# A key's low part copied or subtracted twice, and the values' weights split on VectorE instead of GpSimd

## The chip, the cores and the metric

The kernel runs on one core of a Trainium2 chip. Its metric is the device time of one execution in microseconds (us), given as the median of several runs. Besides the runs there is one profiled execution, whose trace has every instruction of every engine: TensorE (PE in the profile, with its weight loads as PEld), VectorE (DVE), ScalarE (ACT), GpSimd (POOL) and the queue that issues the transfers (SP).

## The reference

Two layers work on 512 latent tokens with a prefix of 256 context tokens, all 1024 wide. Layer 0 mixes tokens with attention, layer 1 with a state space scan in two directions, and each is followed by a gated feed-forward part with a short convolution. The change lies in the attention of layer 0:

```python
q_l, k_l, v_l = jnp.split(h_lat @ w_qkv, [Q_DIM, Q_DIM + KV_DIM], axis=-1)
q_l = rms_norm(q_l.reshape(bsz, seq, N_HEADS, HEAD_DIM), q_norm)
k_l = rms_norm(k_l.reshape(bsz, seq, N_KV_HEADS, HEAD_DIM), k_norm)
q_l = apply_rope(q_l, cos, sin)
k_l = apply_rope(k_l, cos, sin)
...
k_all = jnp.concatenate([k_l, k_c], axis=1)
v_all = jnp.concatenate([v_l, v_c], axis=1)
# per block of queries: softmax(q k^T / 8) v, with 16 query heads on 4 key heads of 64
```

Latent queries see all 768 keys, context queries the 256 of the context. Everything is float32.

## The kernel before

**Numbers in two parts.** TensorE works on a rounded type (fp32r). To keep float32 accuracy each operand is split into a high part, which is a rounded copy of it made on ScalarE (a cast), and a low part, which is the operand minus the high part. `split` (lines 81 to 87) does both: the cast on ScalarE is L85, the subtraction is L87, on VectorE or, with `lo_engine="pool"`, on GpSimd. `mm3` (L105, L106, L108) then adds three matmuls: high by high, high by low, low by high. `load_w` transfers one tile of weights of 128 by 1024 from HBM (L95, issued by SP) and splits it; the tile and its two parts (`wst`, `wh`, `wl`) come out of one pool of ten buffers that is also used by the modulation's weights (`wada`) and the queries' weights (`wq`).

**Who sets the order.** A first section of `attention` is ordered by hand (`manual_schedule`, for PE, ACT and DVE). In it the modulation of the latent and context tokens (L312 on VectorE, L321 on ScalarE, L322 on VectorE, for each of eight rows of 128 channels) runs one row ahead of the projections of the keys and the first queries (`k_step`, six accumulators `ps_l`). All other instructions are put in order by a planner, engine by engine, by when it expects their inputs to be there and by their place in the program; each engine and each DMA queue then works strictly in that order. `pin=True` in `load_w` adds `keep_in_program_order` to the cast and the subtraction: each then has to follow the instruction that was traced before it on its engine.

**After the hand-ordered section.** A loop over six tiles (`for n, j in enumerate(...)`, L744 on) projects the context tokens into one PSUM bank each (`ps_c`, matmuls as `k_step`) and copies the bank out on ScalarE (L748). A pool of four banks serves `ps_c`, the sums of squares of the norms (`ssq`, L567) and later the values (`ps_v`). Into this loop the program puts other work: the two tiles of the values' weights (`wv`), and from n = 1 and n = 2 on the first keys and the first queries (`early`), one step of each per turn.

`keys` and `queries` share `normed`: squares on ScalarE (L558), the gain (L559), a swap of halves by four transfers (L562, `qsw`), sums on TensorE (L567), the rotary product on VectorE (L569, L570, L571), the inverse root in three steps on ScalarE (L576, L577, L578), its correction on VectorE (L580) and the products L581 and L582. `queries` ends with a `split` of 768 columns. `keys` ends with the part that the change touches: a key head lies in one half of the partitions (`s`), and the scores need it in both halves. For each of the two heads of a tile, ScalarE writes the high part to its own half and to the other one (L593, L594), VectorE subtracts the low part in its own half (L595), and ScalarE copies that to the other half (L596). `keys` runs twice: for tile 0 in the loop above, and for tile 1 in the middle of attention (`chain["k"]`).

Behind the loop come the values (`values`, L547: 24 matmuls for each of six tiles of tokens, copied out by L549), between which the row maxima of the first pair of heads are put (`maxima`, L651 on TensorE, L653 on VectorE); the maxima read the queries' and the keys' high parts. Then attention proper follows, eight pairs of heads in seven steps each, with the later queries, the modulation of the later parts and the output projection woven in by costs.

Of the kernel before, what the change touches and what calls it, by code (L numbers as in the profile page):

```python
# [11 lines left out]
ALU = mybir.AluOpType  # L12
# [55 lines left out]
def t3(g, name, dt=F32, n=T):  # L68
    return g.t3p.tile([P, n], dt, tag="t3", bufs=g.n3, name=name)


def t4(g, name, dt=F32):
    return g.p.tile([P, 1024], dt, tag="t4", bufs=10, name=name)


def _r(ap):

    return ap.bitcast(F32)


def split(g, src, hi, lo, lo_engine="dve", pin=False):

    nc = g.nc
    keep = g.tc.keep_in_program_order if pin else lambda i: i
    keep(nc.scalar.copy(hi, src))  # L85
    eng = nc.vector if lo_engine == "dve" else nc.gpsimd
    keep(eng.tensor_tensor(lo, src, _r(hi), ALU.subtract))  # L87


def load_w(g, dram, lo_engine="dve", pin=False):  # L90

    st = t4(g, "wst")
    wh = t4(g, "wh", F32R)
    wl = t4(g, "wl", F32R)
    g.nc.sync.dma_start(st, dram)  # L95
    split(g, st, wh, wl, lo_engine=lo_engine, pin=pin)
    return wh, wl
# [312 lines left out]
def attention(g, adas, project, X):  # L410


    nc, I = g.nc, g.I
# [77 lines left out]
    def k_step(m, j, out, h):  # L491
        ks = slice(j * P, (j + 1) * P)
        mm3(g, tuple(w[:, ks] for w in slabs[m]), [(out, h[m])], m == 0, m == KT - 1)
# [42 lines left out]
    wv = []  # L536
# [18 lines left out]
    def normed(qs, gain):  # L555

        sq = t3(g, "qsq")
        nc.scalar.activation(sq, qs, AF.Square)  # L558
        nc.scalar.activation(qs, qs, AF.Identity, scale=gain)  # L559
        sw = t2("qsw")  # L560
        for b in range(4):
            nc.sync.dma_start(sw[32 * (b ^ 1) : 32 * (b ^ 1) + 32], qs[32 * b : 32 * b + 32, :L])  # L562
        ss = []
        for c0, c1 in ((0, L), (L, T)):
            ps = Bk("ssq")
            for s in S64:
                nc.tensor.matmul(ps[s, : c1 - c0], g.ones[s, :HD], sq[s, c0:c1], start=True, stop=True)  # L567
            ss.append((ps[:, : c1 - c0], slice(c0, c1)))
        nc.vector.tensor_tensor(qs[:, :L], qs[:, :L], g.cos, ALU.mult)  # L569
        nc.vector.tensor_tensor(sw, sw, g.sin, ALU.mult)  # L570
        nc.vector.tensor_tensor(qs[:, :L], qs[:, :L], sw, ALU.add)  # L571
        yield

        y, u = t3(g, "qy"), sq
        for ps, c in ss:
            nc.scalar.activation(y[:, c], ps, AF.Ln, scale=1.0 / HD, bias=eps64)  # L576
        nc.scalar.activation(y, y, AF.Exp, scale=-0.5)  # L577
        nc.scalar.activation(u, y, AF.Square)  # L578
        for ps, c in ss:
            nc.vector.scalar_tensor_tensor(u[:, c], ps, HD * EPS, u[:, c], ALU.add, ALU.mult)  # L580
        nc.vector.tensor_tensor(qs, qs, y, ALU.mult)  # L581
        nc.vector.scalar_tensor_tensor(qs, u, -3.0 * HD, qs, ALU.add, ALU.mult)  # L582
        yield
# [3 lines left out]
    def keys(j, qs):  # L587
        yield from normed(qs, kn)
        for e in range(2):

            h, l = t3(g, f"kh{j}{e}", F32R), t3(g, f"kl{j}{e}", F32R)
            s, o = S64[e], S64[1 - e]
            nc.scalar.copy(h[s], qs[s])  # L593
            nc.scalar.copy(h[o], qs[s])  # L594
            nc.vector.tensor_tensor(l[s], qs[s], _r(h)[s], ALU.subtract)  # L595
            nc.scalar.copy(l[o], _r(l)[s])  # L596
            k2[2 * j + e] = (h, l)

    qprep = {}
# [1 line left out]
    def queries(p, qs):  # L601
        yield from normed(qs(), g.qn8)
        qprep[p] = t3(g, "qh", F32R), t3(g, "ql", F32R)
        split(g, qs(), *qprep[p])
# [139 lines left out]
    for n, j in enumerate((0, 1, 2, 4, 5, 3)):  # L744
        ps = Bk("ps_c")
        for k in range(KT):
            k_step(k, j, ps[:, :C], hc)
        nc.scalar.copy(raw[j][:, L:], ps[:, :C])  # L748
        if n in (1, 3):
            wv.append(load_w(g, I["wv"][len(wv)], lo_engine="pool", pin=True))  # L750
        if n in (1, 2):
            early.append(keys(0, raw[0]) if n == 1 else queries(0, lambda: raw[1]))
        for gen in early:
            next(gen, None)
# [5 lines left out]
    for p, j in ((1, 2), (2, 4), (3, 5)):  # L760
        qraw[p] = raw[j]
    chain = {p: queries(p, lambda p=p: qraw[p]) for p in range(1, 8)}
    chain["k"] = keys(1, raw[3])

    g.oT = {}
# [603 lines left out]
def body(nc, tc, I, out, dbg=None):  # L1369
# [36 lines left out]
    def project(fs, wo):  # L1406

        for i in range(2):
            for m in range(KT):
                down(g, [wo[f] for f in fs], [g.oT[f] for f in fs], g.mod[0][2], streams, x, [[(i, 0, streams[i][0])]], ms=[m])  # L1410
                yield len(fs) * (0.69 if i == 0 else 0.36)

    attention(g, adas, project, X)
    g.tables = True
    nrm = Norm(g, 0, 4, 3, streams, "f0")
# [135 lines left out]
```

## Time and profile before

| | |
|---|---|
| median of 3 runs | 1911.2 us (1906.7 to 1911.81) |
| profiled execution, its own time | 1909.82 us |
| its span, first to last instruction | 1908.0 us |
| granted clock of TensorE over the span | 0.995 |
| busy: PE, DVE, ACT, POOL | 1864.2, 1321.9, 844.5, 263.8 us |
| HBM traffic | 198.79 MB read, 6.82 MB written, 108 GB/s |

How to read the rows: a row of the order of work gives the start in us from the span's beginning, the duration, the engine, the line of the kernel, the operation, and its output and input tiles by name. What stands in square brackets is how long the engine was idle before it, and what ended that. "x2" are two instructions of a kind in a row, with one common duration. A row of a stretch gives its bounds and length, then the busy time (and count) of PE, PEld, DVE, ACT and POOL, the granted clock as a share of full speed, the busy share of the DMA engines, and GB/s. Matmuls overlap, so that the single ones look longer than the distance from one to the next.

### The profile page before, as it was taken

The page shows a single profiled execution, that of the slowest core. Times are in us where ns is not written, and L with a number is a line of the kernel's source. Part 1 is how long each engine was busy: PE and PEld are TensorE (multiplying, and loading weights), DVE is VectorE, ACT ScalarE, POOL GpSimd, SP SyncE. Part 2 cuts the span into 40 slices and gives each one's busy share as a digit, 9 for nine tenths or more (in the row PEclk, how much of TensorE's full clock was granted, in tenths as well). Part 3 has the DMA queues.
Part 4 walks back from the last instruction along what each step waited for, and adds up shares of the span by engine and source line. Part 5 has one row for each costly group of instructions (what it writes and reads, how often), then busy time and mean ns, then how long its engine had stood idle before and what let it go on. Part 6 is the DMA issues. An engine that isn't in the chain of part 4 may idle for free.

```text
span 1908.0 us, 27239 instructions
## 1 busy us (share of the span) xinstructions
PE 1864.2 (98%) x10696; PEld 1527.1 (80%) x10696; DVE 1321.9 (69%) x1953; ACT 844.5 (44%) x1446; POOL 263.8 (14%) x246
## 2 busy tenths in 40 slices
PE   8899999989999999999989999999999999999999
PEld 6674546588888888888888888888888878888887
DVE  5578989678777777544488867777788466565555
ACT  3645644354122222222266677776666352323331
POOL 2200000031000000000040344344334210000000
PEclk8999999999999999999999999999999999999999
DMA  9123341014433555222223434434443223323232
GB/s 338 56 71 106 111 150 55 7 56 167 136 124 121 174 187 175 67 67 67 66 79 103 116 108 122 122 111 133 122 143 111 89 78 90 99 88 111 88 100 89
DMA packets 73424, 210.00 MB, mean 110 GB/s; under 512 B 8912, under 2 KB 14416, under 8 KB 73168
## 3 DMA queue, kind: packets, MB, share of 16 engines
q1 hardware_dynamic: 73296, 208.26, 35.0%
q8 instruction: 84, 1.38, 0.3%
q14 instruction: 44, 0.36, 0.1%
HBM read 198.79 MB, written 6.82 MB: 108 GB/s over the span
## 4 chain that ended last, share of the span: by engine, by line
PE 79%; DVE 9%; issue 4%; ACT 2%; POOL 1%; DMA 1%; SPq 0%; DVEq 0%; POOLq 0%; ACTq 0%
PE ps_up L106 10%; PE ps_up L108 10%; PE ps_up L105 10%; PE ps_d L105 6%; PE ps_d L108 6%; PE ps_d L106 6%; PE ps_in L108 4%; PE ps_in L106 4%; PE ps_in L105 4%; PE ps_o L687 2%; PE ps_s L723 2%; PE ps_st L1147 2%; DVE ht L312 1%; PE ps_wo L108 1%; PE ps_wo L105 1%
## 5 line engine op out<-in xcount | busy, mean ns | idle before, releaser
L87 DVE TENSOR_TENSOR wl<-wst,wh 128x1024 fp32r<-128x1024 f32 x209 | 260.4, 1246 | 243.3 <-PE ps_up L106 137.5
L85 ACT CAST wh<-wst 128x1024 fp32r<-128x1024 f32 x211 | 221.2, 1049 | 426.5 <-DMA wst<-in_wup 336.9
L106 PE MATMUL ps_up<-hlf,wh 128*128 128x512 f32 x1008 | 357.0, 354 | 0.0
L105 PE MATMUL ps_up<-hhf,wh 128*128 128x512 f32 x1008 | 356.9, 354 | 0.0
L108 PE MATMUL ps_up<-hhf,wl 128*128 128x512 f32 x1008 | 356.8, 354 | 0.0
L105 PEld LDWEIGHTS ps_up<-hhf,wh 128*128 128x128 f32 x1008 | 190.6, 189 | 26.5
L108 PEld LDWEIGHTS ps_up<-hhf,wl 128*128 128x128 f32 x1008 | 190.5, 189 | 26.4
L106 PEld LDWEIGHTS ps_up<-hlf,wh 128*128 128x128 f32 x1008 | 190.6, 189 | 26.2
L105 PE MATMUL ps_in<-hhs,wh 128*128 128x512 f32 (+1 forms) x560 | 204.4, 365 | 0.0
L106 PE MATMUL ps_in<-hls,wh 128*128 128x512 f32 (+1 forms) x560 | 199.4, 356 | 0.0
L108 PE MATMUL ps_in<-hhs,wl 128*128 128x512 f32 (+1 forms) x560 | 198.7, 355 | 0.0
L105 PE MATMUL ps_d<-hdh,wh 128*128 128x512 f32 (+1 forms) x568 | 193.6, 342 | 1.4 <-DVE X L897 1.2
L108 PE MATMUL ps_d<-hdh,wl 128*128 128x512 f32 (+1 forms) x568 | 193.5, 341 | 0.0
L106 PE MATMUL ps_d<-hdl,wh 128*128 128x512 f32 (+1 forms) x568 | 193.0, 340 | 0.3 <-DVE hdl L87 0.3
L897 DVE SCALAR_TENSOR_TENSOR X<-ps_d,mod,X 128x512 f32<-128x512 f32 (+1 forms) x224 | 124.9, 583 | 34.1 <-PE ps_d L108 33.6
L106 PEld LDWEIGHTS ps_d<-hdl,wh 128*128 128x128 f32 x568 | 106.6, 188 | 14.9 <-DVE hdl L87 0.7
L105 PEld LDWEIGHTS ps_d<-hdh,wh 128*128 128x128 f32 x568 | 106.3, 188 | 14.8 <-DVE X L897 1.4
L105 PEld LDWEIGHTS ps_in<-hhs,wh 128*128 128x128 f32 x560 | 105.9, 189 | 15.1 <-issue 1.0
L108 PEld LDWEIGHTS ps_in<-hhs,wl 128*128 128x128 f32 x560 | 105.8, 189 | 14.8
L108 PEld LDWEIGHTS ps_d<-hdh,wl 128*128 128x128 f32 x568 | 106.7, 188 | 13.1
L106 PEld LDWEIGHTS ps_in<-hls,wh 128*128 128x128 f32 x560 | 106.0, 189 | 13.2
L726 ACT ACTIVATE pr<-ps_s 128x1024 f32<-128x1024 f32 x56 | 57.1, 1020 | 97.5 <-PE ps_s L725 95.6
(341 smaller groups left out, 3493.7 us busy)
## 6 DMA issues: line engine op xcount, KB each, us to landing
wst<-in_wup SPq DMA_DIRECT2D x88, 512.0 KB, 3.6
wada<-in_adaT SPq DMA_DIRECT2D x56, 512.0 KB, 4.0
wst<-in_win SPq DMA_DIRECT2D x48, 512.0 KB, 3.7
wst<-in_wdown SPq DMA_DIRECT2D x44, 512.0 KB, 4.1
E<-ad SPq DMA_DIRECT2D x64, 256.0 KB, 6.8
wada<-in_adaB SPq DMA_DIRECT2D x24, 512.0 KB, 4.9
ec<-ead SPq DMA_DIRECT2D x64, 128.0 KB, 5.4
wst<-in_wout SPq DMA_DIRECT2D x16, 512.0 KB, 3.6
```

What stands on the lines that cost most here:

```text
L85: keep(nc.scalar.copy(hi, src))
L87: keep(eng.tensor_tensor(lo, src, _r(hi), ALU.subtract))
L105: mm(out, wh, ah, start=first, stop=False)
L106: mm(out, wh, al, start=False, stop=False)
L108: mm(out, wl, ah, start=False, stop=last)
L312: nc.vector.scalar_tensor_tensor(t[:, c0:c1], ap, g.moda[layer][ca][:, m, v : v + 1], rs[:, c0:c1], ALU.mult, ALU.mult)
L687: nc.tensor.matmul(po[S64[e], :n], v, pr[:, 512 * e + off : 512 * e + off + n], start=first, stop=last)
L723: nc.tensor.matmul(outs[e], a[S64[e], k], b[S64[e], q], start=i == 0, stop=False)
L726: nc.scalar.activation(pr, ps, AF.Exp)
L897: nc.vector.scalar_tensor_tensor(ap, o[:, c0:c1], gate[:, m, v : v + 1], ap, ALU.mult, ALU.add)
L1147: nc.tensor.matmul(ps[:, d * 256 : (d + 1) * 256], Bt[:, t * P : (t + 1) * P], xw[d][t], start=t == ts[0], stop=t == ts[-1])
```

## The change

For the half of the partitions that a key does not lie in, the low part is subtracted on VectorE a second time, from the same inputs, instead of being copied there by ScalarE. In the loop over the context tiles, the two loads of the values' weights stand at n = 3 and n = 5 instead of 1 and 3, their subtraction is on VectorE instead of GpSimd, and neither cast nor subtraction is pinned.

```diff
@@ -592,8 +592,8 @@
             s, o = S64[e], S64[1 - e]
             nc.scalar.copy(h[s], qs[s])
             nc.scalar.copy(h[o], qs[s])
-            nc.vector.tensor_tensor(l[s], qs[s], _r(h)[s], ALU.subtract)
-            nc.scalar.copy(l[o], _r(l)[s])
+            for to in (s, o):
+                nc.vector.tensor_tensor(l[to], qs[s], _r(h)[s], ALU.subtract)
             k2[2 * j + e] = (h, l)
 
@@ -746,8 +746,8 @@
         for k in range(KT):
             k_step(k, j, ps[:, :C], hc)
         nc.scalar.copy(raw[j][:, L:], ps[:, :C])
-        if n in (1, 3):
-            wv.append(load_w(g, I["wv"][len(wv)], lo_engine="pool", pin=True))
+        if n in (3, 5):
+            wv.append(load_w(g, I["wv"][len(wv)]))
         if n in (1, 2):
             early.append(keys(0, raw[0]) if n == 1 else queries(0, lambda: raw[1]))
         for gen in early:
```

## The prediction

> **What bounds the kernel.** I read the busy times first, then the busy times of short stretches around the changed lines, then the order of work on each engine there.
>
> ```profile
> PE 1864.2 (98%) x10696; PEld 1527.1 (80%) x10696; DVE 1321.9 (69%) x1953; ACT 844.5 (44%) x1446; POOL 263.8 (14%) x246
> ```
>
> TensorE is busy for 98% of the span. A change on VectorE, ScalarE or GpSimd is therefore worth only the time that TensorE waits for those engines. The stretches show one such wait beside the change (PE, PEld, DVE, ACT and POOL busy, then the granted clock):
>
> ```profile
> 88.25:93.91 5.66, 0.00 (x0) 0.00 (x0) 1.84 (x4) 5.52 (x9) 0.00 (x0) 0.97 0.00 1
> 93.91:98.31 4.40, 4.40 (x24) 4.27 (x24) 4.25 (x6) 2.73 (x4) 0.00 (x0) 0.65 0.00 0
> 98.31:118.66 20.35, 19.80 (x149) 16.72 (x149) 15.95 (x23) 8.70 (x14) 0.00 (x0) 1.00 0.25 75
> ```
>
> TensorE does nothing for 5.66 us, while ScalarE works through nearly all of it. Then 24 matmuls of the values run at a clock of 0.65. From 98.31 on TensorE is nearly full again. The first matmul after the gap says what it waited for:
>
> ```profile
> 93.91 0.58 PE L547 MATMUL ps_v<-wh,hha 128*128 128x256 f32 x1 [5.66 <-ACT raw L748]
> ```
>
> It needs a PSUM bank that holds a finished context projection, and ScalarE's copy (L748) frees it. The copy is late because of what stands ahead of it on ScalarE:
>
> ```profile
> 82.62 0.83 ACT L593 CAST kh<-raw 64x768 fp32r<-64x768 f32 x1 [3.66 <-DVE raw L582]
> 83.36 0.36 ACT L748 COPY raw<-ps_c 128x256 f32<-128x256 f32 x1
> 83.62 1.05 ACT L85 CAST wh<-wst 128x1024 fp32r<-128x1024 f32 x1
> 84.70 0.83 ACT L594 CAST kh<-raw 64x768 fp32r<-64x768 f32 x1
> 88.29 0.83 ACT L596 CAST kl<-kl 64x768 fp32r<-64x768 f32 x1 [2.76 <-DVE kl L595]
> 89.13 0.83 ACT L593 CAST kh<-raw 64x768 fp32r<-64x768 f32 x1
> 89.99 0.83 ACT L594 CAST kh<-raw 64x768 fp32r<-64x768 f32 x1
> 90.83 1.05 ACT L576 ACTIVATE qy<-ssq,eps 128x512 f32<-128x512 f32 x2
> 91.90 0.83 ACT L596 CAST kl<-kl 64x768 fp32r<-64x768 f32 x1
> 92.76 0.84 ACT L577 ACTIVATE qy<-qy 128x768 f32<-128x768 f32 x1
> 93.51 0.35 ACT L748 COPY raw<-ps_c 128x256 f32<-128x256 f32 x1
> ```
>
> The first copy of a low part (L596) waits 2.76 us for VectorE's subtraction L595. Everything behind it on ScalarE waits too, the copy at 93.51 among it. VectorE and GpSimd at that time:
>
> ```profile
> 83.89 0.69 DVE L569 TENSOR_TENSOR raw<-raw,cs 128x512 f32<-128x512 f32 x1 [1.36 <-DMA qsw<-raw]
> 84.50 0.68 DVE L570 TENSOR_TENSOR qsw<-qsw,cs 128x512 f32<-128x512 f32 x1
> 85.11 3.15 DVE L595 TENSOR_TENSOR kl<-raw,kh 64x768 fp32r<-64x768 f32 x1
> 88.19 0.67 DVE L571 TENSOR_TENSOR raw<-raw,qsw 128x512 f32<-128x512 f32 x1
> 90.00 0.96 DVE L595 TENSOR_TENSOR kl<-raw,kh 64x768 fp32r<-64x768 f32 x1 [1.14 <-ACT kh L593]
> 93.63 0.96 DVE L581 TENSOR_TENSOR raw<-raw,qy 128x768 f32<-128x768 f32 x1 [2.68 <-ACT qy L577]
> 94.70 1.02 DVE L580 SCALAR_TENSOR_TENSOR qsq<-ssq,qsq 128x512 f32<-128x512 f32 x2
> 95.76 0.96 DVE L582 SCALAR_TENSOR_TENSOR raw<-qsq,raw 128x768 f32<-128x768 f32 x1
> ```
>
> ```profile
> 84.81 2.64 POOL L87 TENSOR_TENSOR wl<-wst,wh 128x1024 fp32r<-128x1024 f32 x1 [7.58 <-ACT wh L85]
> ```
>
> The same subtraction takes 3.15 us beside GpSimd's L87 and 0.96 us alone, and it ends when that L87 has ended (85.11 + 3.15 = 88.26; 84.81 + 2.64 = 87.45). So all three parts of the edit stand in this wait: ScalarE's L596, GpSimd's L87, and ScalarE's L85 at 83.62.
>
> **The change, part by part.** I follow two chains to 98.31, where the maxima of the first pair start on TensorE: the PSUM bank for the first values, and the first query's high part, which the maxima read.
>
> ScalarE, up to the bank. Gone are L85 at 83.62 (84.70 - 83.62 = 1.08), the wait and the first L596 (89.13 - 85.53 = 3.60, where L594 ends at 84.70 + 0.83), and the second L596 (92.76 - 91.90 = 0.86): 5.54 us. The copy then ends at 93.86 - 5.54 = 88.32 where it ended at 93.86. TensorE has finished its own work at 88.25, so 0.1 us of the 5.66 is left.
>
> The clock. With no gap, the 24 matmuls need 4.40 x 0.65 = 2.86 us, and end at 88.35 + 2.86 = 91.2.
>
> VectorE, up to the query. It now has four L595 (3.84 us at 0.96) where two were. Its work from the first high part (82.62 + 0.83 = 83.45) on is these, the three rotary steps L569 to L571 (0.69 + 0.68 + 0.67 = 2.04), L581 (0.96), L580 (1.02) and L582 (0.96): 8.82 us, to 92.3. L577 on ScalarE, which L581 needs, ends by 92.76 + 0.84 - 5.54 = 88.1, and L581's turn comes at 83.45 + 3.84 + 2.04 = 89.3, so ScalarE is no longer what counts. The cast of the query to its high part follows, 768 columns wide as L593 is, so 0.83 us. This gives 92.3 + 0.83 = 93.1 for the maxima. TensorE, done with the first values at 91.2, then waits 1.9 us in front of them, if its order stays. What is late next is thus VectorE, and the stretch from 98.31 on starts 5.2 us earlier.
>
> Before this point two more things go:
>
> ```profile
> 79.80 0.39 PE L105 MATMUL ps_c<-hha,wsh 128*128 128x256 f32 x1 [0.56 <-DVE qsq L580]
> ```
>
> ```profile
> 73.64 1.05 ACT L85 CAST wh<-wst 128x1024 fp32r<-128x1024 f32 x1
> ```
>
> The first values' cast stands at 73.64 in ScalarE's norm chain of the key. VectorE's L580, and behind it TensorE's fourth context projection, wait for that chain. Without the 1.05 us the 0.56 us wait goes and the key is ready as much earlier. I count 0.6 (bounds 0 and 1.05). The gain at the maxima is then 5.8.
>
> The moved split is two DMA issues, two casts on ScalarE (1.05 each, the rows of L85 above) and two L87, which VectorE does for all other weights already:
>
> ```profile
> L87 DVE TENSOR_TENSOR wl<-wst,wh 128x1024 fp32r<-128x1024 f32 x209 | 260.4, 1246 | 243.3 <-PE ps_up L106 137.5
> ```
>
> So the two cost VectorE 2.5 us in place of GpSimd's 2.64 for one. Without the pin nothing holds the casts behind the context copies. A row on ScalarE shows what the planner does with an instruction whose input is there early:
>
> ```profile
> L628 ACT CAST onesr<-ones x1: 298/298/298, 2.0 to 2.0; 128x128 fp32r<-128x128 f32 x1
> ```
>
> L628 is traced after the hand-ordered section and runs ahead of it, at 2.0 us. The queue of the transfers:
>
> ```profile
> 29.88 0.33 SPq L95 DMA_DIRECT2D wst<-in_wv  x1
> 30.92 8.46 SPq L122 DMA_DIRECT2D wada<-in_adaA  x9
> 72.95 2.50 SPq L562 DMA_DIRECT2D qsw<-raw  x4
> 75.55 0.53 SPq L95 DMA_DIRECT2D wst<-in_wv  x1
> ```
>
> ```profile
> wst<-in_wv SPq DMA_DIRECT2D x1, 512.0 KB, 8.1
> ```
>
> The first transfer is issued at 29.88 and lands at about 38.0. So I expect the splits not later but earlier than now, in gaps of ScalarE and VectorE before 82, wherever the program has them. I take 0 us for them, since ScalarE stands idle 4.49 and 2.82 us before these two casts of the hand-ordered section:
>
> ```profile
> 36.52 0.72 ACT L321 ACTIVATE hha<-ht,mod 128x512 fp32r<-128x512 f32 x1 [4.49 <-DVE ht L312]
> ```
>
> ```profile
> 42.70 0.72 ACT L321 ACTIVATE hha<-ht,mod 128x512 fp32r<-128x512 f32 x1 [2.82 <-DVE ht L312]
> ```
>
> The second transfer, now at 75.55 between the swaps of key and query, may move past both on SP; each swap issues 0.5 us sooner or later by it, which I count at nothing, as VectorE's total and not the swap's landing sets the query. If the cover of the gaps is missing, the cost is two L87 on the VectorE chain, 2.5 us.
>
> The second keys. The same edit there adds two subtractions to VectorE and takes two copies from ScalarE:
>
> ```profile
> 207.26 1.93 DVE L595 TENSOR_TENSOR kl<-raw,kh 64x768 fp32r<-64x768 f32 x2
> ```
>
> ```profile
> 216.91 0.69 DVE L130 COPY ada_sb<-ps_ada 128x512 f32<-128x512 f32 x1 [1.77 <-PE ps_ada L128]
> ```
>
> VectorE has 1.93 us more to do and, ten microseconds on, a pause of 1.77. I count 0.2, with bounds 0 and 1.93 (all of it on TensorE's path).
>
> The sum: 5.2 + 0.6 - 0 - 0.2 = 5.6 us. The profiled execution took 1909.8 us, which is 1.4 below the median of the runs, 1911.2. This makes 1904.2, and I predict 1904.
>
> One price could change this: whether the 1.9 us wait in front of the maxima slows the clock as the 5.66 us gap did. This row pair has a shorter pause of TensorE (0.57 of 2.00 us busy), and the clock stands at 0.50 right behind it:
>
> ```profile
> 150.00:152.00 2.00, 0.57 (x7) 0.20 (x8) 1.91 (x8) 0.00 (x0) 0.00 (x0) 0.90 0.00 0
> 152.00:154.00 2.00, 2.00 (x12) 0.40 (x8) 1.63 (x3) 0.00 (x0) 0.00 (x0) 0.50 0.00 0
> ```
>
> So it may. Some 3 us at half clock would cost 1.5; after a stretch that is full up to 91 I take none, and keep 1.5 as a bound. The Trainium skill, "TensorE: Matmul & The Clock Gate", section "What's actually happening", has the clock halved after an idle window of about 3.4 us. By that rule the sum stays at 1904; by this row pair, which differs from it, it would be 1905.7, and the measurement decides.
>
> **The rivals.** Values first (1902): the planner puts the second values' matmuls ahead of the maxima and the 1.9 us wait is filled. For it: 5 of 6 value tiles are independent work; against it: the present order has the maxima right behind the first tile. 1904.2 - 1.9 = 1902.3.
>
> Splits in the path (1907 to 1908): the splits stay near their place in the program, and two L87 lie ahead of L582: 1904.2 + 2.5 = 1906.7, and 1908.2 with the clock. For it: it is where the program has them; against it: L628.
>
> Too early (1914, slower): the planner expects a transfer sooner than it lands and puts the cast ahead of L321, so that TensorE's next input waits on a DMA. For the first load L321 goes from 36.52 to 38.0 + 1.05, 2.5 us late. The second transfer, behind the nine that end at 39.4, lands at 47.5; a cast ahead of the L321 at 42.70 makes it 5.8 late. With 1.5 for the clock this is 9.8 us against a gain of 5.6: 1914. It decides from 5.6 us on. Against it: the idle 4.49 and 2.82 us, and that such a cast would have to be taken for ready long before it is. A collision of a values' L87 on VectorE with a GpSimd split, priced from L595 at 3.15 - 0.96 = 2.2 us, belongs here. The Trainium skill, "SBUF — State Buffer", section "Who interferes with whom", says that a VectorE instruction with two SBUF inputs and a GpSimd one that reads SBUF shut each other out. The 3.15 us agrees; by that rule a moved L87 can meet any GpSimd split that is left.
>
> Swallowed (1909): the planner's new order in attention gives the gain back: the second keys' 1.93 us land on TensorE's path, and three waits of about 1 us, like the 1.77 above, come with them (1904.2 + 1.7 + 3 = 1909). Against it: VectorE, at 69% of the span, is not what TensorE mostly waits for.
>
> **How the numbers follow.** Forecast 0.42 (1902 to 1906), values first 0.13, splits in the path 0.22, too early 0.10, swallowed 0.13. The range runs from 1899 to 1911, and leaves out most of "too early" and little else. A difference of 0.3%, about what a measurement of this kernel can tell from none, is at 1905.5 seen from the median. Faster by more: most of the forecast and all of values first, 0.50. Slower by more (above 1917): part of the last two, 0.08. The rest, 0.42, is the same.
>
> **What would show it.** The 5.66 us gap before the first values is under 0.5 and their clock near 1.00; four L595 of 0.96 each; no L596; no GpSimd split after 70 us; a wait of 1 to 2 us in front of the first maxima, on the query's cast. Wrong it is if ScalarE waits for a values' transfer before 62, if TensorE's first values wait on a values' L87, or if the stretch from 118.66 to the end grows.

## The result and the profile after

The changed kernel takes 1931.5 us (median; 1927.12 to 1934.62) where the kernel before takes 1908.55 us beside it (six executions, the three of the table above among them): a ratio of 1.0116, 95% interval [1.0098, 1.0134]. It is slower by 1.2%. Its profiled execution took 1930.89 us, with a span of 1929.1, which is 21.1 more than the 1908.0 of before.

The busy times of the changed kernel's page hardly differ from those of before:

```profile
PE 1866.8 (97%) x10696; PEld 1528.7 (79%) x10696; DVE 1324.8 (69%) x1959; ACT 841.5 (44%) x1442; POOL 258.7 (13%) x244
```

TensorE is busy for 2.6 us more in a span that is 21.1 longer. So most of the loss is a wait, and it has to be found by place. These are stretches of the changed kernel (bounds, length, busy PE, PEld, DVE, ACT, POOL, granted clock, DMA share, GB/s):

```profile
17.50:39.40 21.90, 1.26 (x12) 0.19 (x4) 1.23 (x2) 1.72 (x3) 0.00 (x0) 0.50 0.87 327
39.40:46.00 6.60, 6.03 (x16) 4.65 (x17) 2.78 (x8) 1.91 (x4) 1.83 (x1) 0.53 0.71 228
...
87.70:113.20 25.50, 24.81 (x180) 21.08 (x179) 12.20 (x19) 18.17 (x34) 2.96 (x4) 1.00 0.16 42
113.20:116.10 2.90, 2.90 (x26) 2.82 (x24) 2.69 (x5) 2.07 (x4) 0.00 (x0) 1.00 0.00 0
116.10:118.35 2.25, 0.14 (x4) 0.02 (x2) 1.32 (x3) 1.27 (x3) 0.00 (x0) 1.00 0.00 0
118.35:138.20 19.85, 19.84 (x150) 16.76 (x150) 16.38 (x23) 8.26 (x13) 0.00 (x0) 1.00 0.10 22
138.20:433.90 295.70, 286.31 (x1786) 170.42 (x1786) 241.94 (x359) 141.88 (x202) 10.07 (x12) 0.99 0.25 81
433.90:1929.10 1495.20, 1472.99 (x8211) 1273.11 (x8210) 1013.90 (x1470) 642.22 (x1137) 229.11 (x211) 1.00 0.36 111
```

The same stages of the kernel before, cut at the same instructions (the first context projection to the first values, the first scores to the first gate projections, and the rest):

```profile
62.10:93.91 31.81, 24.88 (x179) 21.13 (x177) 13.99 (x19) 22.82 (x40) 8.00 (x6) 0.99 0.28 83
118.66:413.00 294.34, 284.92 (x1786) 169.22 (x1785) 240.23 (x357) 143.46 (x204) 10.08 (x12) 0.99 0.25 81
413.00:1908.00 1495.00, 1473.21 (x8211) 1273.49 (x8210) 1014.62 (x1470) 641.97 (x1137) 228.79 (x211) 1.00 0.36 111
```

The first context projection starts at 87.70 where it started at 62.10, 25.6 us later. From there to the first values it takes 25.50 where it took 31.81, and to the first scores 50.50 (138.20 - 87.70) where it took 56.56 (118.66 - 62.10): 6.1 are won. Attention gives 1.4 back (295.70 for 294.34) and the rest 0.2. 25.6 - 6.1 + 1.4 + 0.2 = 21.1. The gain at the changed lines is there; a loss four times as large stands in front of them, in a stretch whose lines the diff does not touch.

TensorE does almost nothing for 20 us from 17.50 on, and its first matmul after that names its releaser. ScalarE's order of work, and then SP's, show the cause, all of the changed kernel:

```profile
39.40 0.79 PE L105 MATMUL ps_l<-hha,wsh 128*128 128x512 f32 x1 [20.64 <-ACT hha L321]
```

```profile
13.87 0.82 ACT L85 CAST wsh<-wst 128x768 fp32r<-128x768 f32 x1
37.68 1.04 ACT L85 CAST wh<-wst 128x1024 fp32r<-128x1024 f32 x1 [23.00 <-DMA wst<-in_wv]
38.63 0.72 ACT L321 ACTIVATE hha<-ht,mod 128x512 fp32r<-128x512 f32 x1
...
45.24 0.72 ACT L321 ACTIVATE hha<-ht,mod 128x512 fp32r<-128x512 f32 x1 [4.69 <-DVE ht L312]
45.87 1.04 ACT L85 CAST wh<-wst 128x1024 fp32r<-128x1024 f32 x1
```

```profile
29.57 10.83 SPq L95 DMA_DIRECT2D wst<-in_wv  x2
40.49 1.32 SPq L122 DMA_DIRECT2D wada<-in_adaA  x3
```

Before, ScalarE went from the same cast of 0.83 us to the first L321:

```profile
13.53 0.83 ACT L85 CAST wsh<-wst 128x768 fp32r<-128x768 f32 x1
17.73 0.72 ACT L321 ACTIVATE hha<-ht,mod 128x512 fp32r<-128x512 f32 x1 [3.37 <-DVE ht L312]
...
23.57 0.72 ACT L321 ACTIVATE hha<-ht,mod 128x512 fp32r<-128x512 f32 x1 [3.92 <-DVE ht L312]
```

The cast of the first values' weights now comes next on ScalarE at 14.7 (13.87 + 0.82), when its transfer has not even been issued. It stands there for 23.00 us until the data land at 37.68, and the first L321 behind it, which TensorE needs for its first projections, comes at 38.63 instead of 17.73: 20.9 of the 25.6 us. The other 4.7 come in the seven L321 that follow: the first of them comes 6.61 us behind the one in front of it (45.24 - 38.63), where it came 5.84 behind before (23.57 - 17.73), and TensorE runs at 0.53 of its clock behind the gap. The stretch from the first projection of the section to its end, first of the changed kernel, then of the one before, splits them:

```profile
39.40:87.70 48.30, 45.12 (x257) 32.78 (x258) 27.16 (x61) 18.47 (x35) 13.93 (x10) 0.90 0.37 120
18.50:62.10 43.60, 42.54 (x256) 30.74 (x257) 24.20 (x58) 16.56 (x33) 13.99 (x10) 0.96 0.61 230
```

TensorE is idle for 3.2 us of it instead of 1.1, and is busy 2.6 us longer with the same projections, at a clock of 0.90 instead of 0.96: 2.1 + 2.6 = 4.7. The modulation's transfers that stand behind the values' in SP's queue also come later (40.49 for 30.92), since the second values' transfer is issued only at 40.1; but no matmul up to the first scores waits for one of them.

### The profile page after: what moved, and what is told of

It is laid out like the page before. It is cut to its first block, busy times and chain, and to the rows that moved or that the text cites. A ratio compares the mean times of both kernels' runs of the same rounds, so it can differ in the third digit from the quotient of the medians.

```text
span 1929.1 us, 27235 instructions
## 1 busy us (share of the span) xinstructions
PE 1866.8 (97%) x10696; PEld 1528.7 (79%) x10696; DVE 1324.8 (69%) x1959; ACT 841.5 (44%) x1442; POOL 258.7 (13%) x244
## 4 chain that ended last, share of the span: by engine, by line
PE 76%; DVE 12%; issue 4%; ACT 3%; DMA 3%; POOL 2%; SPq 0%; DVEq 0%; POOLq 0%; ACTq 0%
PE ps_up L105 10%; PE ps_up L106 10%; PE ps_up L108 10%; PE ps_d L105 6%; PE ps_d L108 6%; PE ps_d L106 6%; PE ps_in L106 4%; PE ps_in L108 4%; PE ps_in L105 3%; PE ps_o L687 2%; PE ps_s L723 2%; DVE ht L312 1%; PE ps_st L1147 1%; DVE Bf L1077 1%; DVE xf L1077 1%
## 5 line engine op out<-in xcount | busy, mean ns | idle before, releaser
L108 PEld LDWEIGHTS ps_in<-hhs,wl 128*128 128x128 f32 x560 | 105.8, 189 | 14.7
```

Of the source, the lines that this page charges most:

```text
L108: mm(out, wl, ah, start=False, stop=last)
```

## The experiments

The theories, with letters where an expectation uses them. A, the pin: without it the planner puts the cast ahead of the first L321, where ScalarE waits for a transfer. B, crowding: the values' transfers are earlier, and delay the modulation's weights. C: VectorE has more to do. D: what is won before the maxima is given back behind them, by the second keys (D1) or by the order there (D2). E: the early place of the split costs by itself, even with its data there. And two questions: does the gain of 5 to 6 us reach the end without the loss, and which part of the change makes it? Each ratio is to the kernel before on the same chip. The start of the first context projection, of the first scores and of the first gate projections (where attention ends, as in the stretches above) is read from each trace's order of work, and called the section's end, the scores and the end of attention. The section's end of before is 62.1. Each of these times comes from one profiled execution, while executions of one and the same kernel differ by several us (29 of the kernel before on one chip took 1904.78 to 1915.27, at granted clocks of 0.991 to 0.996). A difference of 1 or 2 us in a stage is therefore not yet a difference between kernels; the medians are.

**The kernel before without its pin.**

```diff
-            wv.append(load_w(g, I["wv"][len(wv)], lo_engine="pool", pin=True))
+            wv.append(load_w(g, I["wv"][len(wv)], lo_engine="pool"))
```

> The kernel before with the pin alone taken away: subtraction on GpSimd, n = 1 and 3, the key's low part copied by ScalarE. Theory A: the cast again stands ahead of the first L321, TensorE waits 20 us at 18 to 39, and without the keys' gain of 5 us the time is 1930 to 1937, ratio 1.011 to 1.015. Theory C, or a theory that the later place in the program is the cause: 1908 to 1912, ratio 1.00.

Measured: 1933.44 us, 1.0125 [1.0111, 1.0139]. ScalarE shows the same wait:

```profile
37.97 1.04 ACT L85 CAST wh<-wst 128x1024 fp32r<-128x1024 f32 x1 [23.72 <-DMA wst<-in_wv]
```

Dropping the pin alone, with GpSimd and the places n = 1 and 3 kept, gives the whole loss. The later place in the program is not needed for it.

**The changed kernel with its pin.**

```diff
-            wv.append(load_w(g, I["wv"][len(wv)]))
+            wv.append(load_w(g, I["wv"][len(wv)], pin=True))
```

> The change as it is, but the cast and the subtraction of the values' weights are pinned behind what is traced before them (the pin of the kernel before, on VectorE and at n = 3 and 5). Theory A (the loss of 21 us is the unpinned cast that stands ahead of the first L321 and waits for its transfer until 37.7): the hand-ordered section is as before (last L321 at 62.7), the maxima start at about 93 to 94 instead of 98.3, and the time is 1903 to 1906, ratio 0.997 to 0.999. Theory B (the second transfer of values' weights and the first of the later queries' weights, which moved to 30 to 52, crowd out the modulation's transfers): these move back too, same numbers. Theory C (VectorE's added work, two L87 and four L595, is what costs): still about 1930, ratio 1.011.

Measured: 1911.96 us, 1.0018 [1.0008, 1.0028]. The section ends at 62.9. What TensorE waits for between 62 and 140 (us in all, times, longest):

```profile
PE ps_m L651 <- ACT qh L85: 1.8, 1, 1.8
PE ps_v L547 <- ACT wh L85: 1.5, 1, 1.5
```

The 21 us are gone, so A stands from both sides, and C is not their cause, since VectorE's extra work is all still there. But nothing is gained over before either; the kernel is 0.2% slower, where 1903 to 1906 was expected. The wait of 5.7 has shrunk to 1.5 + 1.8, the first scores come 54.6 us after the section's end (56.6 before), and attention takes 296.8 us (294.3 before; the part on the prediction comes back to this).

**The splits held behind the hand-ordered section, without the pin.**

```diff
-        nc.scalar.copy(raw[j][:, :L], pl[j])
+        last = nc.scalar.copy(raw[j][:, :L], pl[j])
...
-            wv.append(load_w(g, I["wv"][len(wv)]))
+            with g.tc.issue_after(last.ins):
+                wv.append(load_w(g, I["wv"][len(wv)]))
```

> The change as it is, but the loads' ScalarE instructions may not come ahead of the last copy of the latent accumulators (L535), and are free behind it. Theory A: the cast no longer stands in the hand-ordered section, last L321 at 62.7, and the casts fill ScalarE's idle time behind it, so that no L87 is in the query's chain: maxima at 92 to 93, 1902 to 1904, ratio 0.996 to 0.998, some 1 us under the pinned form. Theory C: about 1930.

Measured: 1910.59 us, 1.0012 [1.0002, 1.0021]; the section ends at 63.7. The values' casts stand at 72.52 and 80.29, without a wait. But the next cast that nothing holds, that of a query's weights (L610), now waits for its transfer in the keys' chain:

```profile
86.96 1.05 ACT L85 CAST wh<-wst 128x1024 fp32r<-128x1024 f32 x1 [2.51 <-DMA wst<-in_wq]
```

TensorE waits 4.7 us in front of the maxima in this kernel, and the 1902 to 1904 that were expected are missed. It is the same fault, smaller.

**The splits without their transfer.** In the first version the splits read a tile that is there from the start, so that the values come out of other numbers, and the transfers stay.

```diff
-            wv.append(load_w(g, I["wv"][len(wv)]))
+            i = len(wv)
+            st, wh, wl = t4(g, "wst"), t4(g, "wh", F32R), t4(g, "wl", F32R)
+            nc.sync.dma_start(st, I["wv"][i])
+            two = lambda t: t.rearrange("p (a b) -> p a b", a=2)
+            split(g, X[:, 2 * i : 2 * i + 2, :L], two(wh), two(wl))
+            wv.append((wh, wl))
```

> The change as it is, with the two transfers left as they are, but the splits read two tiles of X, which are there from 5 us on, instead of what the transfers bring (so the values come out of other weights). The unpinned casts still run early, but wait for nothing. Theory A: the 20.6 us wait goes, and of the 4.6 us that the hand-ordered section lost besides, what came from the cold clock goes too; last L321 at 63 to 66, time 1904 to 1909, ratio 0.997 to 1.000. Theory B: the transfers are as crowded as in the changed kernel, last L321 at 66 or later and time 1908 or more. Theory C: about 1930.

Measured: 1928.14 us, 1.0097 [1.0083, 1.0111]. ScalarE:

```profile
14.89 1.04 ACT L85 CAST wh<-X 128x1024 fp32r<-128x1024 f32 x1
...
41.90 1.05 ACT L85 CAST wh<-X 128x1024 fp32r<-128x1024 f32 x1 [20.61 <-DMA wst<-in_wv]
```

The first cast, now that it waits for nothing, runs at 14.89: this is the place that the planner gives it in this kernel. The second still waits for a values' transfer that it does not read. That this comes through the shared ring of buffers is argued, not shown. So the run did not take the wait away, and the next one leaves the two transfers out (no `st`, and no `dma_start`):

> The change with the two transfers of the values' weights left out and the splits reading two tiles of X that are there from 5 us on (the values come out of other weights). In the run before this one of that kind the second cast still waited for a transfer, through the buffer that the transfer wrote. Theory A (the wait for the transfer is the price, not the early place nor the work): TensorE's wait of 20.6 us is gone, the first context projection starts at 63 to 66 instead of 87.7, and the time is 1902 to 1907, ratio 0.996 to 0.999. Theory E (the casts and L87 in the hand-ordered section cost by themselves, through VectorE's chain to each row): first context projection later than 68.

Measured: 1909.86 us, 0.9999 [0.9989, 1.0010]; the section ends at 66.7, between what A (63 to 66) and E (later than 68) gave, and the fault has passed on once more, to the query's weights ahead of the fourth L321:

```profile
41.00 1.04 ACT L85 CAST wh<-wst 128x1024 fp32r<-128x1024 f32 x1 [7.41 <-DMA wst<-in_wq]
```

Pinning that cast too (`split(g, wq[p], wh, wl, pin=p == 4)`) leaves an early split and no wait:

> As the run without the two transfers of the values' weights (splits read X; the values come out of other weights), and the cast of the fourth query's weights pinned to its place, since in that run it had become the one that went ahead: it waited 7.4 us for its own transfer before the fourth L321. Theory A (only a cast that waits for a transfer costs): the first context projection starts at 62 to 64, the first scores 54 us or less behind it, and the time is 1902 to 1906, ratio 0.996 to 0.998. Theory E (casts and L87 in the hand-ordered section cost by themselves): it starts at 65 or later.

Measured: 1910.82 us, 1.0005 [0.9996, 1.0014]. Both values' casts still run early, ahead of the first L321 at 17.80, and the section ends at 62.6:

```profile
9.92 1.03 ACT L85 CAST wh<-X 128x1024 fp32r<-128x1024 f32 x1
...
16.45 1.04 ACT L85 CAST wh<-X 128x1024 fp32r<-128x1024 f32 x1 [2.13 <-POOL wsl L87]
```

So an early split costs nothing that this run can tell when its data are there (62.6 for 62.1). E falls. The scores come 52.1 us after the section's end here, 4.5 earlier than before, and attention takes 299.0, 4.7 more than before: in this execution the gain is lost again behind it, and the median misses the 1902 to 1906 that were expected.

**Early transfers, late splits.** Both transfers stand ahead of the loop, the splits behind the section, the query's weights pinned, and the second keys as before.

```diff
+    wvst = [t4(g, "wst") for _ in range(2)]
+    for i in range(2):
+        nc.sync.dma_start(wvst[i], I["wv"][i])
...
-            wv.append(load_w(g, I["wv"][len(wv)]))
+            wv.append((t4(g, "wh", F32R), t4(g, "wl", F32R)))
+            with g.tc.issue_after(last.ins):
+                split(g, wvst[len(wv) - 1], *wv[-1])
```

> Both transfers of the values' weights are issued early, as in the changed kernel, but the splits are kept behind the hand-ordered section (on ScalarE) and are free there; the fourth query's split pinned to its place; first keys on VectorE, second keys as before. Theory B (the early second transfer crowds out the modulation's): the first context projection starts at 66 or later. Theory A: 62 to 64; the splits fall into VectorE's idle 11 us ahead of the keys, the first scores come 50 to 53 us after the first context projection (56.6 before), and the time is 1902 to 1906, ratio 0.996 to 0.998, unless attention gives some of it back by the clock (1.7 us a step).

Measured: 1909.52 us, 1.0000 [0.9989, 1.0011]; the section ends at 64.0. SP issues both at 30, ahead of the modulation's weights:

```profile
30.01 1.31 SPq L749 DMA_DIRECT2D wst<-in_wv  x2
```

B falls as the cause of the 21 us: with both transfers early, and no cast behind them in front of L321, the section is at most 2 us later than before; it ends at 63.9 also in the kernel below that moves no transfer at all (VectorE for GpSimd, pinned). The scores come 53.0 us after it, 3.6 earlier than before, but attention takes 297.8, 3.5 longer, and the 1902 to 1906 that were expected are missed.

**The keys alone.** The first part of the diff, with the loads as before; then the same for the first keys only, with the second keys' copies (L596) kept.

> The first hunk alone: the low part of the other half is subtracted by VectorE, for both key tiles; the values' weights are split as before (GpSimd, pinned, n = 1 and 3). Theory A (the early cast is the whole loss; the keys' edit by itself is a gain near the maxima): the wait of 5.7 us before the first values falls to about 1, L595 beside GpSimd's L87 still takes 3.1 us, maxima 3 us earlier counted from the first context projection. If that reaches the end, 1905 to 1907, ratio 0.998. Theory D (what is gained before the maxima is given back behind them, as the pinned form showed, where 5.0 us at the maxima were 2.0 at the first scores and nothing at the end): ratio 1.000 to 1.002, 1908 to 1912.

> As the run with the first hunk alone, but the second key tile, in the middle of attention, keeps ScalarE's copy (L596). Theory D1 (the loss behind the maxima comes from the second keys' two more subtractions on VectorE): 2 us under the run with both tiles, 1904 to 1907, ratio 0.997 to 0.999. Theory D2 (it comes from the order and the transfers behind the first keys, not from the second keys): the same as with both tiles within 0.1%.

Measured: 1911.69 us, 1.0014 [1.0004, 1.0023], and 1909.1 us, 0.9995 [0.9985, 1.0005]. VectorE and TensorE's longest wait, with all keys changed:

```profile
85.21 3.17 DVE L596 TENSOR_TENSOR kl<-raw,kh 64x768 fp32r<-64x768 f32 x1
...
89.01 2.89 DVE L596 TENSOR_TENSOR kl<-raw,kh 64x768 fp32r<-64x768 f32 x3
91.93 1.23 DVE L87 TENSOR_TENSOR wl<-wst,wh 128x1024 fp32r<-128x1024 f32 x1
```

```profile
PE ps_m L651 <- ACT qh L85: 5.6, 1, 5.6
```

The wait of 5.7 in front of the values is gone, and one of 5.6 in front of the maxima has taken its place: VectorE is late with the query, by the subtractions (one still 3.17 beside GpSimd's split) and by a split that comes before L581. The first scores come 56.3 us after the section's end, as before (56.6). The two kernels differ by the second keys alone; their medians differ by 2.6 us (0.0019 in the ratio), with intervals that just touch. That is about the difference that D1 gave (2 us), though 1909.1 lies above its 1904 to 1907; I take the second keys to cost something like that, not more surely.

**VectorE for GpSimd, pinned.** First with the first keys' second subtraction, then alone.

```diff
-            wv.append(load_w(g, I["wv"][len(wv)], lo_engine="pool", pin=True))
+            wv.append(load_w(g, I["wv"][len(wv)], pin=True))
```

> The run with the first keys alone, and the values' weights split on VectorE instead of GpSimd, pinned at n = 1 and 3 as before: the change without the later place and without the loss of the pin. If GpSimd's share matters (L595 at 3.15 us beside it, 0.96 alone), the first scores come 1 to 3 us earlier after the first context projection than the 56.6 of that run, and the ratio is 0.997 to 0.999. If VectorE's two L87 (2.5 us) eat that, 56 to 57 and a ratio of 0.999 to 1.001.

> The kernel before, with one part of the change alone: the subtraction of the values' weights is on VectorE; the loads stay at n = 1 and 3 and pinned, and the keys' low parts are still copied by ScalarE. If VectorE's 3.15 us subtraction was long because of GpSimd's split beside it, the first subtraction takes 0.96 us, ScalarE's 2.76 us wait for it shrinks to about 0.6, and the 5.66 us gap before the first values falls to about 3.5. VectorE gets one values' split of 1.25 us in the same stretch, ahead of the query, so the maxima come 1 to 2 us earlier at the most. At the end: the theory that a local gain carries through gives 1908 against 1909.5 of the kernel before (ratio 0.999); the rival that attention gives such gains back, as it did with the keys alone, gives 1909.5 to 1911 (ratio 1.000 to 1.001).

Measured: 1907.03 us, 0.9990 [0.9980, 1.0000], and 1907.17 us, 0.9992 [0.9981, 1.0003]. VectorE, ScalarE and TensorE in the second:

```profile
86.60 0.94 DVE L595 TENSOR_TENSOR kl<-raw,kh 64x768 fp32r<-64x768 f32 x1
```

```profile
87.58 0.84 ACT L596 CAST kl<-kl 64x768 fp32r<-64x768 f32 x1 [0.27 <-DVE kl L595]
```

```profile
PE ps_v L547 <- ACT raw L748: 3.2, 1, 3.2
```

With GpSimd out of the way the subtraction takes 0.94 instead of 3.15, ScalarE's wait for it 0.27 instead of 2.76, and TensorE's wait 3.2 instead of 5.7. The first scores come 54.2 us after the section's end, 2.4 earlier than before; with the first keys' edit as well, 54.0. That edit adds nothing here that the run can tell.

**Everything that helped, together.** The splits held as above, the query's weights pinned, the first keys only.

> A form meant to keep the gain: splits of the values' weights on VectorE and free behind the hand-ordered section but not in it, the split of the fourth query's weights pinned to its place (in the run that only moved the values behind the section it went ahead of the keys and waited 2.5 us for its transfer on ScalarE), the first key tile's low part subtracted twice, the second key tile as before. Theory A with D1: maxima 5 to 6 us earlier than before counted from the first context projection, 1902 to 1905, ratio 0.996 to 0.998. Theory D2: ratio 0.999 to 1.001.

Measured: 1908.69 us, 1.0000 [0.9991, 1.0009]. The scores come 53.4 us after the section's end, 3.2 earlier than before; attention takes 297.9, 3.6 longer, in a profiled execution that was the slowest of its eleven (1912.64 us). No version is faster than the kernel before beyond doubt; the two with VectorE for GpSimd come nearest, by 0.1%, with intervals that reach 1.0000 and 1.0003.

## Why the prediction was wrong

**The step that failed** is the price of the moved split: "So I expect the splits not later but earlier than now, in gaps of ScalarE and VectorE before 82 ... I take 0 us for them." They did come earlier, and the first values' cast came too early: at 14.7, when the rows quoted for it (a transfer issued at 29.88, landing at 38.0) already said that it could not run before 38. The argument took the idle 4.49 and 2.82 us in front of the L321 at 36.52 and 42.70 for the gaps that the cast would fill, that is, it let the cast wait for its data and then look for a gap. ScalarE worked in its fixed order and did not look for one: it stood for 23.00 us. The price of a wrong place is the whole time until the data land. Why the planner put the cast there, no run shows. L628 at 2.0 us, which was read as a reason for a free ride, was the warning: an unpinned instruction can go ahead of the entire section.

**The rival "too early"** had the mechanism, and its mark in the trace (ScalarE waiting for a values' transfer before 62), but not the size. It let the cast slip in front of the L321 of 36.52, 2.5 us late; it went in front of the one of 17.73, 20.9 us late. Its argument against itself was that such a cast would have to be taken for ready long before it is; the place at 14.7, with data at 37.68, looks like just that. Its other parts, 5.8 us for the second transfer and a collision with GpSimd, are not in the trace as such: the second cast stands at 45.87, behind an L321, and in the run with both transfers early no such delay shows.

**What was right** is the part that was worked out from rows. ScalarE and VectorE around the maxima, and TensorE's waits from 113 to 120, of the changed kernel:

```profile
110.51 0.84 ACT L594 CAST kh<-raw 64x768 fp32r<-64x768 f32 x1
111.25 0.36 ACT L748 COPY raw<-ps_c 128x256 f32<-128x256 f32 x1
```

```profile
109.56 0.94 DVE L596 TENSOR_TENSOR kl<-raw,kh 64x768 fp32r<-64x768 f32 x1
...
111.14 0.95 DVE L596 TENSOR_TENSOR kl<-raw,kh 64x768 fp32r<-64x768 f32 x1
112.33 1.92 DVE L596 TENSOR_TENSOR kl<-raw,kh 64x768 fp32r<-64x768 f32 x2 [0.23 <-PE ps_c L108]
114.33 0.96 DVE L581 TENSOR_TENSOR raw<-raw,qy 128x768 f32<-128x768 f32 x1
```

```profile
PE ps_m L651 <- ACT qh L85: 2.1, 1, 2.1
```

Between L594 and the copy L748 no copy of a low part is left; the four subtractions (L596 is their line now) take 0.94 to 0.96 each; TensorE has no wait in front of the first values, and their 24 matmuls take the stretch 113.20:116.10, 2.90 us at full clock (2.86 expected). VectorE is late next, and TensorE waits 2.1 us for the query's cast, where 1.9 was expected. The maxima come 30.65 us after the first context projection (118.35 - 87.70), where they came 36.21 after it (98.31 - 62.10): 5.6 us, against 5.8. The 2.1 us wait did not slow the clock (1.00 in 118.35:138.20), so the price of 1.5 kept as a bound was not due. That looks like luck: a wait of 2.2 us at the same place cost 1.7 us in the kernel without the transfers (last section).

**What would have been short even with a pin.** The sum let 5.6 us go through to the end. With the pin back, the first scores gain 2.0, attention gives 2.5 back, and the ratio is 1.0018. These are attention with the pin, and attention with the first keys alone:

```profile
117.50:414.30 296.80, 287.06 (x1786) 170.43 (x1786) 242.01 (x359) 142.06 (x202) 10.08 (x12) 0.99 0.25 81
```

```profile
120.60:411.10 290.50, 283.12 (x1786) 169.12 (x1786) 240.09 (x357) 143.60 (x204) 10.06 (x12) 1.00 0.25 82
```

The same 1786 matmuls keep TensorE busy for 287.06 us with the pin, 284.92 before and 283.12 with the first keys alone, and its idle time with the pin is nearly that of before (9.7 for 9.4). So 2.1 of the 2.5 us are not waits of TensorE but matmuls that take longer. Most of it is the clock: TensorE runs at half clock for about 3.4 us at two places of attention with the pin, at one before (the row pair of the prediction), and at none with the first keys alone. That may belong to the execution and not to the kernel. The medians show that the 5.6 us do not reach the end; where they go is shown only in part. "Swallowed", priced at 1909, gives about the time of the pinned change. Of its causes the second keys are borne out (about 2.6 us between the medians of two runs), the three added waits in attention are not. Why attention takes 290.5 to 299.0 us in these kernels, with nearly the same work in it, is not settled beyond this.

## What to carry to other kernels

A constraint that keeps an instruction in its place may be the only thing that holds it behind its data: before it is dropped, find the first place where the order could put that instruction, and price the move from there to the landing of its transfer (here 14.7 to 37.68), not from the gap that one hopes it fills. An engine that works in order charges that wait to everything behind it, and fixing one such instruction can hand the fault to the next free one. A local gain of 5 us in a kernel whose busiest engine is at 98% has to be read again at the next stage, since a wait removed on one engine can stand, at nearly the same length, in front of the next product. Gains of 1 to 2 us are read from medians, not from the stages of one execution.

## What was not expected of the hardware

The clock's loss after a short pause comes in lumps, or not at all. Two kernels at the same place of attention, first with the first keys' edit, then with VectorE for GpSimd alone:

```profile
150.60:152.60 2.00, 0.97 (x9) 0.33 (x5) 1.91 (x7) 0.64 (x2) 0.00 (x0) 1.00 0.00 0
152.60:154.60 2.00, 1.56 (x16) 0.42 (x16) 2.00 (x5) 0.00 (x0) 0.00 (x0) 1.00 0.00 0
154.60:156.60 2.00, 2.00 (x19) 1.07 (x15) 2.00 (x4) 1.03 (x1) 0.00 (x0) 1.00 0.73 188
```

```profile
149.00:151.00 2.00, 0.57 (x7) 0.21 (x9) 1.91 (x7) 0.00 (x0) 0.00 (x0) 1.00 0.00 0
151.00:153.00 2.00, 2.00 (x16) 0.35 (x8) 1.76 (x4) 0.00 (x0) 0.00 (x0) 0.60 0.00 0
153.00:155.00 2.00, 2.00 (x11) 0.86 (x9) 1.27 (x3) 0.55 (x1) 0.00 (x0) 0.55 0.73 254
```

TensorE is idle for 1.47 us in the one (1.03 + 0.44) and keeps its clock. In the other it is idle for 1.43 in the first of the three stretches, and the clock falls to half for about 3.4 us, a loss of 1.7 (0.40 and 0.45 of 2.00 us). Yet the 2.1 us wait in front of the changed kernel's maxima, behind a stretch that was full, cost nothing. The kernel without the transfers and with the query's weights pinned has nearly the same wait at the same place, also behind a stretch that was full:

```profile
91.10:93.30 2.20, 0.04 (x1) 0.00 (x0) 1.30 (x3) 1.21 (x3) 0.00 (x0) 1.00 0.00 0
93.30:99.30 6.00, 5.93 (x29) 3.66 (x30) 3.70 (x5) 4.52 (x6) 0.00 (x0) 0.72 0.30 61
```

There the six microseconds behind it run at a clock of 0.72, a loss of 1.7 us. The Trainium skill, "TensorE: Matmul & The Clock Gate", section "What's actually happening", lets the clock be set window by window of about 3.4 us, with windows that run on regardless of the kernel. The length of the slow phase agrees with it, and free windows would explain why nearly equal pauses end differently; that a pause of 1.4 us is enough is more than its rule of an idle window says. No run here moved a pause against the window to test it.
